# Where the tiles of a matmul begin in their partition: two paddings in a ten-layer kernel

## The chip, the cores and the metric

The kernel runs on one core of one Trainium2 chip. The metric is the device time of a run in microseconds (us), lower being better; the time given for a kernel is the median of several runs. A matmul here takes one operand that is held in the array (stationary, loaded by a weight load, "PEld" in the profile) and one that streams through it (moving). Both come from SBUF, whose 128 partitions each hold a row of bytes; a tile has the same byte address in every partition, and this document is about that address.

## The reference

A sequence of 256 tokens of width 1024 goes through two blocks of two layers each. Everything is float32.

```python
x = first_block(x, ...)    # 2 x (rmsnorm, mixer, + x; rmsnorm, swiglu, + x)
                           #   layer 0: gated spatial mixing beside latent attention
                           #   layer 1: retention with four heads
x = second_block(x, ...)   # 2 x (swiglu with 4096, layer norm; hybrid mixer, layer norm; swiglu, layer norm)
# hybrid mixer: a gated delta rule behind a causal convolution of 4 taps,
# a chunked attention with a relative bias, and a sliding-window attention with sinks,
# each gated and projected, then one output projection
```

Almost all of the arithmetic is in products of the 256 tokens with large weight matrices.

## The kernel before, in words

The work is a chain of ten stages: the two mixers and two feed-forwards of the first block, then feed-forward, hybrid mixer, feed-forward twice for the second. The order of the work is written out by hand; there is no loop on the chip. The same code runs once without a chip to record which slabs of weights are needed in which order, and then again to emit the instructions.

Each float32 product is made of three fast ones: both operands are split in two parts, "hi" (rounded to the fast format float32r) and "lo" (the rest), and `mm3` (line 230) issues hi x hi, hi x lo and lo x hi into the same PSUM tile. All matmuls go through `mm` (line 227), so all of them have line 228 in the profile; transposes through `tr` (line 235, 236 in the profile).

The weights stream in units of up to 1 MB. `prep` (line 135) loads each half of a unit into a tile "raw" through SyncE's DMA queue, has ScalarE round it into "hi" and VectorE subtract into "lo"; up to four units are ahead of their use, on four buffers each of hi and lo.

The activations stand transposed in two tiles "xh" and "xl" of 8 x 256 (`new_xT`, line 427), one pair per stage. Products appear in three forms:
- features by tokens (`pair_tiles`, line 339, and `chunk` in `ffn`, line 587): the weights are stationary, 256 columns of xh or xl move. In the hybrid mixer the branch projections use the same form with the branch's own transposed output, a tile "s", moving.
- tokens by features (`block`, line 284): xh or xl is stationary, up to 512 columns of weights move.
- the second matrix of a feed-forward and the output projections (`emit_down`, line 616, `outlast`, line 370): a pair of tiles "s" is stationary, 512 columns of weights move into four PSUM tiles "acc".

Attention, retention and the delta rule use plain float32 matmuls on smaller tiles between these.

SBUF is handed out from pools, in the order in which `build` (line 1530) opens them. The constants come first (`consts`, line 1512): the identity (512 bytes of each partition), the masks (3584), a column of -0.5 (64) and "colt", the small per-feature columns, 196 numbers wide (784 bytes). Then the weights' pool with hi, lo and raw, then the pool of the working tiles, then xh and xl. In the working pool `tile` (line 204) picks the smallest of six sizes; all of a size stand together, in the order in which the sizes are first used: 4096 bytes (11 of them), 64 (24), 2048 (22), 1088 (4), 256 (10), 2080 (2). The last, "s2x", are used by the convolution of the hybrid mixer alone (`cb_conv`, line 1095), which takes 518 numbers of one. The allocator rounds each tile up to a multiple of 32 bytes; the first constant stands at byte 16512. The profile strips the digits from the names, so the sizes "s4", "s2", "s1" all appear as "s", and "s2x" as itself.

Of the kernel before, what the change touches and what calls it, by code (L numbers as in the profile page):

```python
# [4 lines left out]
F32 = mybir.dt.float32  # L5
# [10 lines left out]
HEAD = 2  # L16
TAIL = 3
ACC = 4


class Nothing:
# [94 lines left out]
class Net:  # L116
# [13 lines left out]
        self.hold = False  # L130
        self.pend = {}

    # weight stream

    def prep(self):
        i = self.made
# [62 lines left out]
        self.nc.sync.dma_start(t, self.dram[name][:, o:o + n])  # L199
        return t  # L200

    # tiles

    def tile(self, *free, dt=F32):
        n = int(np.prod(free))
        for tag, size, bufs in (("c", 16, 24), ("c2", 64, 10), ("s1", 272, 4), ("s2", 512, 22), ("s2x", 520, 2), ("s4", 1024, 11)):
            if n <= size:
                break
        else:
            raise ValueError(n)  # L210
        t = self.sp.tile([128, size], dt, tag=tag, bufs=bufs, name=tag)
        t = t[:, 0:n]
        if len(free) == 2:
            t = t.rearrange("p (a b) -> p a b", a=free[0])
        elif len(free) == 3:
            t = t.rearrange("p (a b c) -> p a b c", a=free[0], b=free[1])
        return t
# [4 lines left out]
    def work(self):  # L222
        return self.pp.tile([128, 512], F32, tag="work", bufs=8 - ACC, name="work")

    # short forms

    def mm(self, out, l, r, start=True, stop=True):
        self.nc.tensor.matmul(out, lhsT=l, rhs=r, start=start, stop=stop)  # L228
# [43 lines left out]
        self.nc.gpsimd.tensor_tensor(out=out, in0=out, in1=self.nh[:, 0:n], op=ALU.pow)  # L272

    def bc(self, a, m):
        """[128, n] -> [128, n, m] with a stride of zero"""
        return a.unsqueeze(2).to_broadcast([128, a.shape[1], m]) if not self.recording else a

    def bh(self, a, h):
        """[128, n] -> [128, h, n] with a stride of zero"""
        return a.unsqueeze(1).to_broadcast([128, h, a.shape[1]]) if not self.recording else a  # L280

    # products with streamed weights

    def block(self, b, n, units, xT, cb):
        ps = self.acc() if self.gacc else self.work()
# [10 lines left out]
        yield  # L296

    def group(self, n, units, xT, cb):
        """out[token, n columns] of x @ w, one block of tokens after the other"""
        self.need_x(1)  # L300
        for b in range(2):
            yield from self.block(b, n, units, xT, cb)
        self.pump()

    def opening(self, groups):
        """the first groups of a stage: the second block of tokens comes late"""
        groups = [(n, self.col_units(key, cols), cb) for n, key, cols, cb in groups]
        self.need_x(0)
        for b in range(2):
            for n, units, cb in groups:  # L310
                for i, _ in enumerate(self.block(b, n, units, self.xT, cb)):
                    if b == 0 and i == 0 and units is groups[-1][1]:
                        self.need_x(1)
                    yield

    def col_units(self, key, cols, K=8, per=4):
        """cols: column ranges, or a function of the inputs that gives the [K * 128, n] slab"""
        units = []
        n = sum(c1 - c0 for c0, c1 in cols)
        for k in range(0, K, per):  # L320
            def fn(inp, k=k):
                return kslab2(key(inp), k, k + per, *cols)
            units.append(self.unit((per, n), fn) + (per,))
        return units
# [3 lines left out]
        yield from self.group(n, self.col_units(key, cols, K, per), self.xT, cb)  # L328

    def apair(self, key, cols, cb):  # L330
        """out[feature, token] of x @ w for two tiles of features"""
        def fn(inp):
            return kslab2(key(inp), 0, 8, *cols)
        u = self.unit((8, 256), fn)
        self.need_x(1)
        yield from self.pair_tiles(u, 0, self.xT, 8, cb)
        self.pump()
# [10 lines left out]
        yield  # L348

    def outproj(self, key, r0, xT, y, first, last, K=4, per=2):  # L350
        """y[block][half] += x @ w for K tiles of the rows of w from r0"""
        units = []
        for k in range(0, K, per):
            def fn(inp, k=k):
                return kslab(key(inp), r0 + k, r0 + k + per, 0, 1024)
            units.append(self.unit((per, 1024), fn))
        for b in range(2):
            for k in range(K):
                hi, lo = units[k // per]
                for n in range(2):  # L360
                    self.mm3(y[b][n], tuple(t[:, k, 128 * b:128 * b + 128] for t in xT),
                             (hi[:, k % per, 512 * n:512 * n + 512], lo[:, k % per, 512 * n:512 * n + 512]),
                             first and k == 0, last and k == K - 1)
                if k % 2 == 1 and k < K - 1:
                    yield ("part", b)
            if b == 1:
                self.pump()
            yield ("block", b)

    def outlast(self, key, r0, xTs, y, first):  # L370
        """y += x @ w for the last rows of w, four tiles per item of xTs; in the last units the first block of tokens comes first"""
        n = 2 * len(xTs)

        def unit(i):
            return self.unit((2, 1024), lambda inp: kslab(key(inp), r0 + 2 * i, r0 + 2 * i + 2, 0, 1024))

        def emit(i, b, w):
            xT = xTs[i // 2]
            xT = xT() if callable(xT) else xT
            for k in range(2):  # L380
                for h in range(2):
                    self.mm3(y[b][h], tuple(t[:, 2 * (i % 2) + k, 128 * b:128 * b + 128] for t in xT),
                             (w[0][:, k, 512 * h:512 * h + 512], w[1][:, k, 512 * h:512 * h + 512]),
                             first and i == 0 and k == 0, i == n - 1 and k == 1)
        for i in range(n - TAIL):
            w = unit(i)
            for b in range(2):
                emit(i, b, w)
                if b:
                    self.pump()  # L390
                yield ("part", b)
        ws = {}
        for b in range(2):
            for i in range(n - TAIL, n):
                if b == 0:
                    ws[i] = unit(i)
                    if i == n - TAIL:
                        self.pump()
                        self.hold = True
                emit(i, b, ws[i])  # L400
                yield ("block", b) if i == n - 1 else ("near" if b and i == n - 2 else "part", b)

    def to_T(self, src, b, dst, n, k0=0):
        """src [128 tokens, n * 128] into dst hi/lo [128, k, 256]"""
        for q in range(0, n, 4):
            m = min(4, n - q)
            ps = self.work()
# [2 lines left out]
            p = ps[:, 0:128 * m].rearrange("p (k t) -> p k t", k=m)  # L410
# [3 lines left out]
    def pair(self, n):  # L414
        return self.tile(n, 256, dt=F32R), self.tile(n, 256, dt=F32R)

    # ends of stages

    def need_x(self, b):
        for i in range(b + 1):  # L420
# [81 lines left out]
        self.pend[b] = post  # L502

    def finish_out(self, b, y):
        """the last layer norm: squares about the mean of the first half, the second half comes last"""
        c = self.how[3]
        z, h, junk = self.tile(1024), self.tile(1024), self.tile(1024)
        sm, q, nm0, nm, dm, e, r = (self.tile(n) for n in (2, 2, 1, 1, 1, 1, 1))
# [34 lines left out]
        for _ in gen:  # L543
            pass

    # the two-matrix gated feed-forward

    def ffn(self, nt, gate, up, down, nxt):
        """gate, up: (fn of inputs -> matrix, first column); down: fn -> matrix"""
        C = nt // 2  # L550
        self.gacc = False
        y = self.new_y()
# [70 lines left out]
        hp, late = head()  # L623
        for c in range(C):
# [3 lines left out]
            if HEAD <= c <= C - TAIL:  # L628
                for e in range(0 if c == HEAD else c - 1, c):
                    w = unit_down(e)  # L630
# [17 lines left out]
                        emit_down(c, b, w, (j,))  # L648
            self.finish(b, y[b])

    # softmax over the last axis of [128, H, K]

    def softmax(self, s, H, K, scale, sink=None):
        """scale: a number, or one per row and head (positive)"""
        nm = self.tile(H)
        self.nc.vector.tensor_reduce(out=nm, in_=s, axis=AX.X, op=ALU.max)
        if sink is not None:
# [17 lines left out]
        return p  # L675

    def p_T(self, p, H, nk):
        """p [128 q, H, nk * 128] -> [128 k, H, nk, 128 q]"""
        pT = self.tile(H, nk, 128)
        flat = pT.rearrange("p a b c -> p (a b c)")  # L680
        for i in range(0, H * nk, 4):
# [7 lines left out]
                self.vcp(flat[:, 128 * i:128 * i + 512], ps)  # L689
        return pT  # L690

    # layer 0 of the first block

    def even(self, nxt):
        self.gacc = True
# [78 lines left out]
        vv = [self.tile(8, 64) for _ in range(2)]  # L774

        def rope(x, b, H, dst):
            """x [128, H, 32]"""
            r = rt1 if b else rt
            pool = self.nc.gpsimd
            t = self.tile(H, 32)  # L780
# [165 lines left out]
        run(fill, 1)  # L946
        self.tail(fill, y)

    # layer 1 of the first block

    def odd(self, nxt):
        w_in = lambda inp: inp["odd_w_in"][0]
# [86 lines left out]
        g = self.outlast(lambda inp: inp["odd_w_out"][0], 8, [oT[2], lambda: oT[3]], y, False)  # L1039
        self.tail(halfway(g, 3, lambda: E(3)), y)  # L1040

    # the mixer of the second block

    def hyb(self, l, nxt):
        nc = self.nc
# [212 lines left out]
        def task_a():  # L1258
            while "kvc" not in events:
                yield "wait"  # L1260
            M = self.masks
            # beta and g
            beta, g = self.tile(2, 4), self.tile(2, 4)
            while "qc" not in events:
                yield "wait"
# [23 lines left out]
                self.mul(t, self.bh(M["U"], 4), self.bc(g[:, b], 128))  # L1289
                gU.append(t)  # L1290
            yield
            # k in token layout, normalised; v in token layout; the lengths of q
            kt, vt, rq = [None] * 2, [None] * 2, [None] * 2

            def lengths(ps):
# [26 lines left out]
                nc.vector.tensor_reduce(out=rq[b], in_=by_head(sq), axis=AX.X, op=ALU.add)  # L1322
                nc.gpsimd.tensor_scalar(out=rq[b], in0=rq[b], scalar1=128e-6, scalar2=128e-12, op0=ALU.mult, op1=ALU.add)
            yield
            # decays: from j to i in [i, j], below the diagonal times beta and with the diagonal
            Dx, DT = [None] * 2, [None] * 2
            for b in range(2):
                ps = self.work()
# [33 lines left out]
                at[b] = DT[b]  # L1362
                self.mul(at[b], DT[b], ps)
            yield
            # inverse of I + A: blocks of four in closed form, then doubled; X = inverse, Y = its transpose
            X, Y, Q = ([self.tile(512) for _ in range(2)] for _ in range(3))
            idb = self.bh(self.ident, 4)
            B, IB, C = Q, X, Y
# [138 lines left out]
        y = self.new_y()  # L1507
        self.tail(self.outlast(lambda inp: inp["w_out_2"][l], 0, mT, y, True), y)

    # the whole  # L1510

    def consts(self):
        nc = self.nc
# [6 lines left out]
        self.nh = self.cp_.tile([128, 16], F32, name="nh")  # L1520
        nc.gpsimd.memset(self.nh, -0.5)
        if not self.recording:
            self.colt = self.cp_.tile([128, max(self.collay.n, 1)], F32, name="colt")

    def late_consts(self):
        nc = self.nc
# [121 lines left out]
```

## Time and profile before

| | |
|---|---|
| runs | 2352.81, 2352.85, 2354.22 us; median 2352.85 us |
| span of the profiled execution (first to last instruction) | 2348.7 us |
| the time of the profiled execution itself | not listed apart from its span; the median of the runs is 4.15 us above the span |
| busy: PE, PEld, DVE, ACT, POOL | 99%, 91%, 59%, 46%, 4% |
| matmuls and weight loads | 15966 each |
| DMA | 419.51 MB, mean 179 GB/s |

PE is the matmul engine, PEld its weight loads, DVE VectorE, ACT ScalarE, POOL GpSimd. A matmul's busy time is longer than the distance from its start to the next one's, because matmuls are pipelined: the distances tell what a matmul costs, not the mean duration. The profile's order of the two inputs in a name is that of the alphabet and doesn't tell which is stationary; the shape does, with the code.

### The profile page before, as it was taken

The page shows a single profiled execution, that of the slowest core. Times are in us where ns is not written, and L with a number is a line of the kernel's source. Part 1 is how long each engine was busy: PE and PEld are TensorE (multiplying, and loading weights), DVE is VectorE, ACT ScalarE, POOL GpSimd, SP SyncE. Part 2 cuts the span into 40 slices and gives each one's busy share as a digit, 9 for nine tenths or more (in the row PEclk, how much of TensorE's full clock was granted, in tenths as well). Part 3 has the DMA queues.
Part 4 walks back from the last instruction along what each step waited for, and adds up shares of the span by engine and source line. Part 5 has one row for each costly group of instructions (what it writes and reads, how often), then busy time and mean ns, then how long its engine had stood idle before and what let it go on. Part 6 is the DMA issues. An engine that isn't in the chain of part 4 may idle for free.

```text
span 2348.7 us, 38487 instructions
## 1 busy us (share of the span) xinstructions
PE 2323.6 (99%) x15966; PEld 2140.5 (91%) x15966; DVE 1393.4 (59%) x1764; ACT 1087.6 (46%) x1530; POOL 92.5 (4%) x149
## 2 busy tenths in 40 slices
PE   8999999999999999999999999999999999999998
PEld 7789988889989999999998999899999999989997
DVE  6654475565455454786666454655457875664544
ACT  6644344354444444564445444444445544453433
POOL 4200000000000000000000000000000000000000
PEclk9999999999999999999999999999999999999999
DMA  7465555555556555553365555555555533665552
GB/s 244 139 206 189 189 193 173 191 170 190 192 171 217 195 184 176 185 174 118 105 201 199 194 183 193 182 201 189 188 181 185 186 105 107 189 206 188 189 189 90
DMA packets 120575, 419.51 MB, mean 179 GB/s; under 512 B 14408, under 2 KB 17224, under 8 KB 120400
## 3 DMA queue, kind: packets, MB, share of 16 engines
q1 hardware_dynamic: 120112, 416.53, 53.7%
q8 instruction: 125, 2.05, 0.3%
q10 hardware_dynamic: 288, 0.52, 0.1%
q14 instruction: 50, 0.41, 0.1%
HBM read 415.95 MB, written 1.05 MB: 178 GB/s over the span
## 4 chain that ended last, share of the span: by engine, by line
PE 97%; DVE 1%; POOL 1%; ACT 0%; DMA 0%; issue 0%; SPq 0%; POOLq 0%; DVEq 0%; ACTq 0%
PE work L228 52%; PE acc L228 42%; PE work L236 2%; DVE lo L148 0%; DMA raw<-in_w 0%; POOL c L271 0%; ACT hi L147 0%; DVE s L251 0%; POOL c L828 0%; POOL c L827 0%; POOL c L272 0%; DVE s L239 0%; PE work L1412 0%; ACT s L258 0%; DVE xl L239 0%
## 5 line engine op out<-in xcount | busy, mean ns | idle before, releaser
L148 DVE TENSOR_TENSOR lo<-raw,hi 128x1024 fp32r<-128x1024 f32 (+3 forms) x772 | 918.3, 1209 | 564.0 <-ACT hi L147 562.3
L147 ACT CAST hi<-raw 128x1024 fp32r<-128x1024 f32 (+3 forms) x772 | 783.4, 1037 | 922.2 <-issue 667.3
L228 PE MATMUL work<-xh,hi 128*128 128x256 f32 x2496 | 699.2, 280 | 0.0
L228 PE MATMUL work<-xl,hi 128*128 128x256 f32 x2496 | 696.5, 279 | 0.0
L228 PE MATMUL work<-xh,lo 128*128 128x256 f32 x2496 | 696.4, 279 | 0.0
L228 PE MATMUL acc<-hi,s 128*128 128x512 f32 (+1 forms) x1736 | 553.4, 391 | 0.0
L228 PEld LDWEIGHTS work<-xh,hi 128*128 128x128 f32 x2496 | 468.5, 188 | 2.7
L228 PEld LDWEIGHTS work<-xl,hi 128*128 128x128 f32 x2496 | 467.1, 187 | 2.7
L228 PEld LDWEIGHTS work<-xh,lo 128*128 128x128 f32 x2496 | 469.1, 188 | 0.0
L228 PEld LDWEIGHTS acc<-hi,s 128*128 128x128 f32 x1736 | 325.7, 188 | 65.8 <-ACT s L261 0.3
L228 PE MATMUL acc<-lo,s 128*128 128x512 f32 (+1 forms) x868 | 337.6, 389 | 0.0
L228 PE MATMUL acc<-xh,hi 128*128 128x256 f32 x800 | 227.5, 284 | 0.0
L228 PE MATMUL acc<-xl,hi 128*128 128x256 f32 x800 | 223.9, 280 | 0.0
L228 PE MATMUL acc<-xh,lo 128*128 128x256 f32 x800 | 223.7, 280 | 0.0
L228 PEld LDWEIGHTS acc<-lo,s 128*128 128x128 f32 x868 | 163.1, 188 | 30.6
L239 DVE TENSOR_TENSOR s<-s,work 128x512 f32<-128x512 f32 (+1 forms) x128 | 81.0, 636 | 172.3 <-PE work L228 160.9
L228 PEld LDWEIGHTS acc<-xh,hi 128*128 128x128 f32 x800 | 150.2, 188 | 0.8 <-issue 0.5
L228 PEld LDWEIGHTS acc<-xl,hi 128*128 128x128 f32 x800 | 150.1, 188 | 0.7 <-issue 0.5
L228 PEld LDWEIGHTS acc<-xh,lo 128*128 128x128 f32 x800 | 150.2, 188 | 0.2
L228 PE MATMUL work<-hi,xh 128*128 128x512 f32 x320 | 128.6, 402 | 0.2 <-ACT xh L261 0.2
L228 PE MATMUL work<-hi,xl 128*128 128x512 f32 x320 | 126.6, 396 | 0.5 <-DVE xl L239 0.5
L228 PE MATMUL work<-lo,xh 128*128 128x512 f32 x320 | 126.5, 395 | 0.0
(117 smaller groups left out, 1949.8 us busy)
## 6 DMA issues: line engine op xcount, KB each, us to landing
raw<-in_w SPq DMA_DIRECT2D x748, 512.0 KB, 4.3
s<-in_rows SPq DMA_DIRECT2D x16, 512.0 KB, 7.4
raw<-in_w SPq DMA_DIRECT2D x12, 288.0 KB, 3.4
s<-in_rows SPq DMA_DIRECT2D x9, 256.0 KB, 5.0
raw<-in_w SPq DMA_DIRECT2D x4, 384.0 KB, 6.8
raw<-in_w SPq DMA_DIRECT2D x4, 256.0 KB, 4.4
s<-in_relb SPq DMA_DIRECT2D x2, 512.0 KB, 4.3
raw<-in_w SPq DMA_DIRECT2D x4, 240.0 KB, 2.5
```

Of the source, the lines that this page charges most:

```text
L147: self.nc.scalar.copy(hi[:, a:b], raw)
L148: self.nc.vector.tensor_tensor(out=lo[:, a:b], in0=raw, in1=hi[:, a:b].bitcast(F32), op=ALU.subtract)
L228: self.nc.tensor.matmul(out, lhsT=l, rhs=r, start=start, stop=stop)
L236: self.nc.tensor.transpose(out, src, self.ident)
L239: self.nc.vector.tensor_tensor(out=out, in0=a, in1=b, op=op)
```

## The change

Two paddings, and comments taken out. The tile for the columns of constants is made wider, up to the next multiple of 512 bytes behind the constants, and only its first part is used, as before. The two buffers of the convolution are made 24 numbers wider. No instruction is added, dropped or moved.

```diff
+LINE = 512
+FIRST = 16512
...
-    # weight stream
+
...
     def tile(self, *free, dt=F32):
         n = int(np.prod(free))
-        for tag, size, bufs in (("c", 16, 24), ("c2", 64, 10), ("s1", 272, 4), ("s2", 512, 22), ("s2x", 520, 2), ("s4", 1024, 11)):
+        for tag, size, bufs in (("c", 16, 24), ("c2", 64, 10), ("s1", 272, 4), ("s2", 512, 22), ("s2x", 544, 2), ("s4", 1024, 11)):
             if n <= size:
                 break
...
         if not self.recording:
-            self.colt = self.cp_.tile([128, max(self.collay.n, 1)], F32, name="colt")
+            fixed = 512 + 3584 + 64 + FIRST
+            self.colt = self.cp_.tile([128, max(self.collay.n, 1) + -(fixed + 4 * self.collay.n) % LINE // 4], F32, name="colt")[:, 0:max(self.collay.n, 1)]
```

## Rows read from the trace of the kernel before

**Rows 1.** The page's opening, busy time by engine, and granted clock in 40 slices.
```profile
span 2348.7 us, 38487 instructions
...
PE 2323.6 (99%) x15966; PEld 2140.5 (91%) x15966; DVE 1393.4 (59%) x1764; ACT 1087.6 (46%) x1530; POOL 92.5 (4%) x149
...
PEclk9999999999999999999999999999999999999999
```

**Rows 2.** PE's waits, longest in total first: us in total, times, longest.
```profile
PE work L236 <- DVE s L251: 10.0, 4, 8.7
PE work L228 <- DVE s L251: 4.0, 1, 4.0
PE work L236 <- POOL s L829: 1.1, 1, 1.1
```

**Rows 3.** The chain in order of time: start us, us, what, xcount.
```profile
143.54 5.45 PE work L228 x48
...
159.89 11.31 PE work L228 x96
...
260.61 22.61 PE work L228 x192
283.22 15.00 PE acc L228 x66
...
2324.13 16.37 PE acc L228 x72
```

**Rows 4.** Groups of PE's instructions, shapes apart: tile<-inputs, shape, xcount | busy us, mean ns.
```profile
L228 PE MATMUL work<-xh,hi 128*128 128x256 f32 x2496 | 699.2, 280 | 0.0
...
L228 PE MATMUL acc<-hi,s 128*128 128x512 f32 x1712 | 546.4, 392 | 0.0
L228 PE MATMUL acc<-lo,s 128*128 128x512 f32 x856 | 333.5, 390 | 0.0
L228 PE MATMUL acc<-xh,hi 128*128 128x256 f32 x800 | 227.5, 284 | 0.0
...
L228 PE MATMUL work<-hi,xh 128*128 128x512 f32 x320 | 128.6, 402 | 0.2 <-ACT xh L261 0.2
...
L228 PE MATMUL acc<-s,hi 128*128 128x256 f32 x384 | 70.5, 285 | 0.0
L228 PE MATMUL acc<-s,lo 128*128 128x256 f32 x192 | 54.5, 284 | 0.0
L228 PE MATMUL acc<-hi,xh 128*128 128x512 f32 x80 | 32.5, 406 | 0.0
```

**Rows 5.** PE's timeline, a branch projection: start us, us, operation, xcount.
```profile
1173.19 0.40 PE L228 MATMUL acc<-s,hi 128*128 128x256 f32 x2
...
1183.62 0.40 PE L228 MATMUL acc<-s,hi 128*128 128x256 f32 x2
```

**Rows 6.** PE's timeline, column groups of the odd layer.
```profile
309.96 0.39 PE L228 MATMUL work<-lo,xh 128*128 128x512 f32 x1
...
323.49 0.39 PE L228 MATMUL work<-hi,xl 128*128 128x512 f32 x1
```

**Rows 7.** PE's timeline, a 264-column group of the hybrid mixer and the next matmul.
```profile
955.52 0.28 PE L228 MATMUL acc<-hi,xh 128*128 128x264 f32 x1
...
958.42 0.39 PE L228 MATMUL acc<-hi,xh 128*128 128x512 f32 x1
```

## The prediction, made before the result was known

> **What bounds the kernel now.** I read the page's first block, then the waits of PE, then the chain of waits in order of time, the groups of PE's instructions with their shapes kept apart, and last PE's timeline in three short stretches.
>
> [...] PE's largest wait is 10.0 us in all, its next 4.0 us [rows 2]. Nearly the whole span is therefore matmuls back to back, and the time is the sum of the distances from one matmul's start to the next. DVE (59%) and ACT (46%) have room, and no wait of PE names a DMA.
>
> The chain gives these distances, since it counts the matmuls of an unbroken stretch: 96 in 11.31 us and 192 in 22.61 us are 117.8 ns each, 48 in 5.45 us are 113.5 ns each, 66 in 15.00 us and 72 in 16.37 us are 227.3 ns each [rows 3]. The first two kinds are 256 columns wide, the last kind 512.
>
> The timeline adds two more. With a tile "s" against "hi" and "lo" at 256 columns (the branch projections), the 87 matmuls from 1173.19 to 1183.62 take 10.43 us, 119.9 ns each [rows 5]. With 512 columns of "hi" or "lo" moving and xh or xl stationary (the column groups of the odd layer), the 58 from 309.96 to 323.49 take 13.53 us, 233.3 ns each [rows 6].
>
> So the same shape costs 117.8 or 119.9 ns, and 227.3 or 233.3 ns, in steady runs. What differs is where the operands lie. From the program's allocation (constants from byte 16512, tiles rounded up to 32 bytes) I work out each tile's start modulo 512: 16512 + 512 + 3584 + 64 + 784 = 21456, rounded to 21472, is 480. All that follows in the pools in multiples of 512 keeps 480: hi, lo, raw, the 4096-byte and the 2048-byte tiles. Behind the four 1088-byte and the two 2080-byte tiles xh and xl start at 210208, which is 288. Slices that a matmul takes are whole multiples of 512 bytes apart, save in the 264- and 288-column units, so a tile's start holds for all of its slices. Moving start minus stationary start is then:
> - 256 columns, xT moving over a weight: 288 - 480 = -192, at 117.8 ns (rarely 113.5)
> - 256 columns, s moving over a weight: 0, at 119.9 ns
> - 512 columns, weight moving over s: 0, at 227.3 ns
> - 512 columns, weight moving over xT: +192, at 233.3 ns
>
> It isn't the accumulator that makes the difference: the 72 matmuls of the last feed-forward stay in one PSUM tile for 18 in a row, the 66 change it after three, and both run at 227.3 ns [rows 3].
>
> **The change part by part.** *The constants.* colt grows from 784 to 832 bytes, so the weights' pool begins at 21504 and hi, lo, raw, s4 and s2 start at 0 instead of 480. *The convolution buffers.* Two tiles grow from 2080 to 2176 bytes; with the four of 1088 they now fill 17 times 512, and xh and xl start at 210432, which is 0 as well. The instructions stay the same in number, shape and order: the load of colt still writes 196 columns, the convolution still uses 518 columns of its tile, no queue and no wait changes, and the stripped comments are nothing. These parts cost 0; what hides even a small change in them is that PE waits for none of these tiles [rows 2]. All the effect there can be is in the matmuls' distances.
>
> *What the matmuls' distances become.* After the change moving and stationary start at the same place everywhere: distance 0, which the trace has in both shapes, only 32 bytes lower in the 512. I take the rows at distance 0 as the nearest:
> - xT moving, 256 columns: 3 x 2496 + 3 x 800 = 9888 matmuls [rows 4]. Five runs of 48 like that in rows 3 and two of 24 are at 113.5 ns, 288 in all; the other 9600 are at 117.8. At 119.9 they cost 9600 x 2.1 ns = +20.2 us and 288 x 6.4 ns = +1.8 us.
> - s moving, 256 columns: 384 + 192 [rows 4], stay at 119.9: 0.
> - s stationary, 512 columns: 1712 + 856 [rows 4], stay at 227.3: 0.
> - xT stationary, 512 columns: 3 x 320 + 3 x 80 = 1200 [rows 4], from 233.3 to 227.3: 1200 x 6.0 ns = -7.2 us.
>
> The sum is +14.8 us, all on the path, since PE has no slack. It is made against the profiled execution: 2348.7 + 14.8 = 2363.5 us of span. Around its span that execution has what the other runs have too: their median of 2352.85 lies 4.15 us above the span, which I carry over unchanged. That gives 2352.85 + 14.8 = 2367.7 us.
>
> *Bounds.* No row shows distance 0 with both starts at 0 of 512, so the price of a 256-column matmul is open between two ends. From below: 227.3 - 119.9 = 107.4 ns is what 256 further columns cost at the same distance, so 12.5 ns of each matmul at distance 0 are not streaming; were all of this gone, and what xT's have on top, it would be 9600 x 10.4 + 288 x 6.1 + 576 x 12.5 + 2568 x 12.5 + 1200 x 18.5 ns = 163 us less. From above: every 512-column matmul at the 233.3 ns of rows 6, and the 256s at 119.9, is 2568 x 6.0 = +15.4 us and no -7.2 us: 14.8 + 15.4 + 7.2 = +37 us. I take the rows at distance 0, since they are the same instructions at the distance that the change sets.
>
> [...]
>
> **A further hint on what matters.** In the 264-column groups the slices of hi and lo lie 1056 bytes apart, so the moving start runs through 480, 0, 32 and 64 over xT's 288. The 24 matmuls from 955.52 to 958.42 take 2.90 us, 120.8 ns [rows 7]; less 8 columns at 107.4 / 256 ns that is 117.4, about the 117.8 of the others. Half of them already start at a multiple of 64, one in four at 0 of 512. An aligned moving start by itself does not show a gain. The stationary start is never aligned in the trace.
>
> **The rivals.**
> 1. *Aligned starts are cheaper in themselves* (faster). A load of 512 bytes that begins at 480 or 288 touches two pieces of 512, at 0 one. If the extra piece is what costs, the 256s may settle at 113.5 ns, the quickest that rows 3 show, and xT's 512s at 227.3: 9600 x 4.3 + 576 x 6.4 + 1200 x 6.0 ns = 41.3 + 3.7 + 7.2 = 52.2 us less, 2301 us. For it: the 113.5 exist at the same starts, so the extra is avoidable. Against: s and xT touch equally many pieces and yet cost differently, and the 264s show nothing.
> 2. *Only the 512s follow the distance*; the 117.8 of the 256s is set by the weight load and stays: -7.2 us, 2345.7 us. For it: the weight load is busy for 91% of the span [rows 1], and a 256-column matmul has little more time than its load. Against: 119.9 with the same load.
> 3. *No effect*, the differences come from something other than starts: 2352.85 us. Against: rows 5 and 6.
> 4. *Slower still*: at 0 both streams hold each other up and the 512s settle at 233.3 everywhere, the upper bound above: 2352.85 + 37 = 2390 us. It decides from the first feed-forward on. Against: 227.3 is steady at distance 0.
>
> **How the numbers follow.** Forecast 0.45, rival 1 0.28, rival 2 0.09, rival 3 0.10, rival 4 0.08. The forecast's own range is 2361 to 2374 us (0.5 ns of reading on 9888 matmuls and a few us of settling at each switch). Rival 1 may come with anything from a quarter of its gain to the full bound, so the range is 2300 to 2386: it leaves out the lower half of rival 1 and most of rival 4. Within 0.2% (4.7 us) is what a measurement can't tell from no change. Faster: rivals 1 and 2, 0.37; same: rival 3, 0.10; slower: forecast and rival 4, 0.53.
>
> **What would show it.** In the chain after, stretches of 96 should take 11.5 us instead of 11.31, those of 66 still 15.0 us; the odd layer's 512s against xT should be at 227 ns, and no run at 113.5 should be left. Rival 1 shows as 96 in 10.9 us or less. If the 66s leave 15.0 us, the place in the 512 counts and not the distance alone, and the step "nearest rows" is wrong. If nothing moves in any of these stretches, rival 3 holds. Any change in the waits of PE beyond a few us would mean that something other than the starts was changed.

## The result and the profile after

The changed kernel takes 2368.36 us (median of four runs, 2367.84 to 2369.13) against 2352.99 us for the kernel before (four runs, 2352.81 to 2354.22): a ratio of 1.0064, with a 95% interval of 1.0050 to 1.0079. It is slower by 15.4 us; 2367.7 was forecast.

The opening of the page, after: span, busy time by engine, granted clock in 40 slices.

```profile
span 2365.8 us, 38487 instructions
...
PE 2340.4 (99%) x15966; PEld 2163.8 (91%) x15966; DVE 1393.5 (59%) x1764; ACT 1087.7 (46%) x1530; POOL 92.7 (4%) x149
...
PEclk9999999999999999999999999999999999999999
```

Against [rows 1] the instruction counts are equal, DVE, ACT and POOL are within 0.2 us, and the granted clock is again at nine tenths or more in all slices. Only PE and PEld grew, by 16.8 and 23.3 us.

The waits of PE, after: us in total, times, longest.

```profile
PE work L238 <- DVE s L253: 10.5, 3, 9.4
PE work L230 <- DVE s L253: 4.0, 1, 4.0
PE work L238 <- POOL s L831: 1.2, 1, 1.2
```

With [rows 2] these make 0.6 us more. So nearly all of the loss lies inside the unbroken stretches of matmuls.

The chain in order of time, after: start us, us, what, xcount.

```profile
144.89 5.75 PE work L230 x48
...
161.55 11.51 PE work L230 x96
...
263.43 23.03 PE work L230 x192
286.46 14.99 PE acc L230 x66
...
2341.33 16.36 PE acc L230 x72
```

Line by line against [rows 3]: 48 matmuls went from 5.45 to 5.75 us (113.5 to 119.8 ns each), 96 from 11.31 to 11.51 (117.8 to 119.9), 192 from 22.61 to 23.03; the 66 and the 72 of 512 columns did not move.

PE's timeline after, in the column groups of the odd layer (the same 58 matmuls as [rows 6]):

```profile
313.01 0.40 PE L230 MATMUL work<-lo,xh 128*128 128x512 f32 x1
...
326.17 0.39 PE L230 MATMUL work<-hi,xl 128*128 128x512 f32 x1
```

13.16 us instead of 13.53: 226.9 ns each instead of 233.3. The branch projections, after, the same 87 matmuls as [rows 5]:

```profile
1180.57 0.40 PE L230 MATMUL acc<-s,hi 128*128 128x256 f32 x2
...
1191.01 0.40 PE L230 MATMUL acc<-s,hi 128*128 128x256 f32 x2
```

10.44 us, 120.0 ns each: unchanged.

For the balance I took all start-to-start distances of a kind from both traces, leaving out those above 148 ns (256 columns) and 276 ns (512 columns), which hold a wait or another instruction:

| kind | number | before, ns | after, ns | sum |
|---|---|---|---|---|
| 256 columns, xT moving over a weight | 9820 | 117.68 | 119.92 | +22.0 us |
| 512 columns, weight moving over xT | 1154 | 233.35 | 227.83 | -6.4 us |
| 512 columns, weight moving over s | 2536 | 227.85 | 227.63 | -0.6 us |
| 256 columns, s moving over a weight | 560 | 119.89 | 119.90 | 0 |

Together +15.0 us; the medians differ by 15.4 us. The two spans differ by 17.1 us. What is more lies mostly in three places outside the table: the first matmul starts at 9.45 us instead of 8.66 (+0.8 us); behind PE's wait of 4.0 us in the first stage the granted clock is 0.50 for 6.8 us instead of 3.4, and 1.00 on both sides of it (+0.9 us); and the 384-column matmuls of the first stage take 0.7 us more. Smaller groups give 0.3 us back. The profiled execution of before was probably also a quick one, which is an estimate: where a run's time stands beside its own span it is 2.6 us above it (2368.41 and 2365.8 here; 2353.0 and 2350.4 for the kernel before in a later run), while the 2348.7 us of [rows 1] lie 4.15 us below the median.

### The profile page after: what moved, and what is told of

It reads as the page before. It is cut to its first block, busy times and chain, and to the rows that moved or that the text cites. A ratio compares the mean times of both kernels' runs of the same rounds, so it can differ in the third digit from the quotient of the medians.

```text
span 2365.8 us, 38487 instructions
## 1 busy us (share of the span) xinstructions
PE 2340.4 (99%) x15966; PEld 2163.8 (91%) x15966; DVE 1393.5 (59%) x1764; ACT 1087.7 (46%) x1530; POOL 92.7 (4%) x149
## 4 chain that ended last, share of the span: by engine, by line
PE 97%; DVE 1%; POOL 1%; ACT 0%; DMA 0%; issue 0%; SPq 0%; POOLq 0%; DVEq 0%; ACTq 0%
PE work L230 52%; PE acc L230 42%; PE work L238 2%; DVE lo L150 0%; DMA raw<-in_w 0%; POOL c L273 0%; ACT hi L149 0%; DVE s L253 0%; POOL c L830 0%; POOL c L829 0%; POOL c L274 0%; DVE s L241 0%; PE work L1414 0%; DVE xl L241 0%; ACT s L260 0%
## 5 line engine op out<-in xcount | busy, mean ns | idle before, releaser
L230 PE MATMUL work<-xh,hi 128*128 128x256 f32 x2496 | 706.7, 283 | 0.0
L230 PE MATMUL work<-xh,lo 128*128 128x256 f32 x2496 | 706.4, 283 | 0.0
L230 PE MATMUL work<-xl,hi 128*128 128x256 f32 x2496 | 706.3, 283 | 0.0
L230 PEld LDWEIGHTS work<-xl,hi 128*128 128x128 f32 x2496 | 478.7, 192 | 2.7
L230 PEld LDWEIGHTS work<-xh,hi 128*128 128x128 f32 x2496 | 478.7, 192 | 2.7
L230 PEld LDWEIGHTS work<-xh,lo 128*128 128x128 f32 x2496 | 478.7, 192 | 0.0
L230 PE MATMUL acc<-xl,hi 128*128 128x256 f32 x800 | 226.7, 283 | 0.0
L230 PE MATMUL work<-s,s 128*128 128x128 f32 (+8 forms) x884 | 122.5, 297 | 4.0 <-DVE s L253 4.0
```

## Experiments

The forecast's theory is called *distance*: what counts is the moving operand's start minus the stationary one's. Its first rival is *place*: what counts is where in 512 bytes each start lies. All kernels are built from the changed kernel, by one to four lines each; the short forms of long lines in the diffs below show only what differs. "x" stands for xh and xl; x at 64 means that both begin at 64 modulo 512, and all other operands at 0 unless it is said. The means are taken as in the table above.

**1. The constants' padding alone** (weights and s at 0, x at 320).

```diff
-("s2x", 544, 2)
+("s2x", 520, 2)
```

> Only the constants' padding: hi, lo and all tiles s start at 0 of 512, xh and xl at 320, so that xT minus weight is 320, which is -192 modulo 512, as before the change. Distance theory (the price of a matmul follows from moving start minus stationary start alone): everything as before the change, 2353 us (2351 to 2355), 96 matmuls in 11.31 us, xT's 512-column matmuls at 233.3 ns. Place theory (a start at 0 of 512 has a price of its own, whatever the other operand does): the 256-column matmuls keep the 119.9 ns of the changed kernel since their weights begin at 0, xT's 512s go back to 233.3: 2368 + 7 = 2375 us.

2352.68 us, ratio 0.9997 (0.9988 to 1.0007). The chain of this kernel:

```profile
160.09 11.31 PE work L230 x96
...
260.81 22.61 PE work L230 x192
283.43 15.01 PE acc L230 x66
```

Every weight and every s is now aligned, and the stretches are those of [rows 3] to 0.01 us. Its timeline in the odd layer, 57 matmuls from first to last start:

```profile
310.16 0.39 PE L230 MATMUL work<-lo,xh 128*128 128x512 f32 x1
...
323.46 0.40 PE L230 MATMUL work<-lo,xh 128*128 128x512 f32 x1
```

13.30 us, 233.3 ns each: also as before [rows 6]. Aligning everything but x did nothing; place, which gave 2375 us, is wrong.

**2. The convolution's padding alone** (all operands at 480, none aligned).

```diff
-            self.colt = self.cp_.tile([128, max(self.collay.n, 1) + -(fixed + 4 * self.collay.n) % LINE // 4], F32, name="colt")[:, 0:max(self.collay.n, 1)]
+            self.colt = self.cp_.tile([128, max(self.collay.n, 1)], F32, name="colt")[:, 0:max(self.collay.n, 1)]
```

> Only the convolution buffers' padding: every tile, xh and xl too, starts at 480 of 512; nothing is aligned, and all distances are 0. Distance theory: as the changed kernel, 2368 us (2366 to 2370), 96 in 11.51 us, xT's 512s at 227.3 ns. Place theory: 480 is as misaligned as before, so as before, 2353 us and 11.31 us.

2369.29 us, ratio 1.0064 (1.0047 to 1.0081). The chain of this kernel:

```profile
145.30 5.75 PE work L230 x48
...
161.96 11.51 PE work L230 x96
...
263.84 23.03 PE work L230 x192
286.88 14.99 PE acc L230 x66
```

These are the durations of the whole change, to 0.01 us, with no tile at a multiple of 512. Over the whole trace the 256s of xT take 119.92 ns on average, xT's 512s 227.95. The whole loss comes from the 192 bytes by which the convolution's buffers push x.

They push x against the weights, but also against "raw", which ScalarE and VectorE read while PE works. The two traces tell these apart: the 256s beside which neither engine worked on "raw" take 117.72 ns before and 119.84 after, those beside which one or both did 117.63 to 117.67 and 119.96 to 119.98. So the 2 ns do not come from the other engines' work on the weights.

**3 and 4. How far does the distance count?** x at 64 and at 128.

```diff
-("s2x", 544, 2)
+("s2x", 552, 2)        # x at 64
+("s2x", 560, 2)        # x at 128
```

> The changed kernel with the convolution buffers 32 numbers wider than before the change instead of 24: xh and xl at 64 of 512, all else at 0. Distance theory with a period of 256 bytes: 64 is the same as -192, so 117.8 ns for the 256s and 233.3 ns for xT's 512s, 2353 us. Distance theory with a period of 512: a distance that no row has; on a straight line through 117.8 at -192 and 119.9 at 0 it is 120.6 ns, and 225 ns for the 512s, 2372 us. Place theory: 2368 us or more.

> xh and xl at 128 of 512, all else at 0. No row has this distance. Distance theory with a straight line: 121.3 ns for the 256s, 223 ns for xT's 512s, 2377 us. [...] Place theory: 2368 us.

x at 64, one run: 2351.76 us beside 2353.42 for the kernel before.

```profile
160.58 11.31 PE work L230 x96
...
283.92 15.01 PE acc L230 x66
```

Means of 117.67 and 233.34 ns, as with x at 320 (117.70 and 233.38): in this pair the price repeats after 256 bytes. So the kernel before stood at distance 64 of 256 (in experiment 1's terms 320 - 256; in the prediction's, -192), and 192 for the 512s.

x at 128, one run: 2371.61 us, expected 2377 by the straight line, 2368 by place.

```profile
162.46 11.52 PE work L230 x96
```

The 256s are at 119.61 ns, back at nearly the price of distance 0, and the 512s at 232.4. Neither of the two gave both.

**5 to 9. The rest of the circle**, with a pad ahead of xh and xl in their pool.

```diff
+self.xp.tile([128, 8], F32, tag="pad", bufs=1, name="pad")   # 32 bytes; 24: 96, 40: 160, 48: 192, 56: 224
```

> xh and xl at 32 of 512, all else at 0. Smooth theory (the price of a matmul is a smooth function of the distance, with a period of 256 bytes): between the neighbours at 0 and 64, 118.9 ns for the 256s and 230 ns for xT's 512s, 2360 us. Step theory (what counts is which pieces of the memory both streams meet in, so neighbours say nothing): anything from 113.5 to 123 ns for the 256s, 2310 to 2400 us, and a value more than 0.5 ns from the middle of its neighbours.

> xh and xl at 96 of 512, all else at 0. Smooth theory: between the neighbours at 64 and 128, 118.7 ns for the 256s and 232.9 ns for xT's 512s, 2361 us. Step theory: anything from 113.5 to 123 ns, more than 0.5 ns from that middle.

> xh and xl at 192 of 512, all else at 0: the mirror of 64, so that xT's 512-column matmuls have the distance -192, the one that the 256s have in the kernel before. Smooth theory: between the known 128 and 256, 119.8 ns for the 256s, 229.9 ns for xT's 512s, 2370 us. [...] Step theory: anything else.

> xh and xl at 224 of 512, all else at 0. Smooth theory: near the price at 256, 119.9 ns for the 256s and 228.6 ns for xT's 512s, 2369 us. Step theory: more than 0.5 ns away from that.

> xh and xl at 160 of 512, all else at 0: the last of the eight distances. Smooth theory: between its neighbours at 128 and 192, 118.1 ns for the 256s and, for xT's 512s at distance 96, between the known 64 and 128, 231.0 ns: 2354 us. Step theory: more than 0.5 ns away from that middle.

One run each: x at 32 2342.32 us, at 96 2375.4, at 192 2334.17, at 224 2360.52 (the kernel before beside them: 2354.26), and at 160 2360.04 (beside 2352.1). A stretch of 96 in each of the five chains, in this order:

```profile
160.88 11.20 PE work L230 x96
```

```profile
160.75 11.52 PE work L230 x96
```

```profile
158.97 11.31 PE work L230 x96
```

```profile
162.34 11.36 PE work L230 x96
```

```profile
161.27 11.40 PE work L230 x96
```

The mean prices, by distance modulo 256 bytes, in ns (the 512s of a kernel stand at 256 minus the distance of its 256s; the period of 256 rests on the one pair 64 and 320):

| distance | 0 | 32 | 64 | 96 | 128 | 160 | 192 | 224 |
|---|---|---|---|---|---|---|---|---|
| 256 columns, x over a weight | 119.9 | 116.8 | 117.7 | 120.0 | 119.6 | 118.5 | 116.6 | 118.3 |
| 512 columns, weight over x | 227.8 | 233.3 | 229.6 | 233.4 | 232.4 | 234.1 | 233.3 | 233.2 |

The smooth curve that I had laid through the first points was missed four times (2360 expected for x at 32, 2361 for 96, 2370 for 192, 2369 for 224); at 160 its 118.1 for the 256s came within 0.5 ns, but its 231.0 for the 512s was off by 2.4. The step theory's claim, more than 0.5 ns off the middle for the 256s, held in four of the five, but it named no value and is not shown by that: the pieces of memory it speaks of were a guess that no run shows, and the highest mean of the 256s is 120.0 ns where its range went to 123. Where x stands decides, by no rule that these runs show: neighbours 32 bytes apart differ by up to 5.5 ns, and the two shapes have their lowest prices at different distances. That only the distance counts, and not x's own place, is shown for the distances 0 and 64 (experiments 1 to 3); at the other six only one place was tried.

**10 and 11. One weight tile moved**: lo at 64, with hi, s and x at 0. "raw" stands behind lo and moves to 64 with it; no matmul reads it.

```diff
+        if i == 0:
+            self.wp.tile([128, 16], F32, tag="pad1", bufs=1, name="pad1")     # ahead of lo
...
+        if i == 0:
+            self.wp.tile([128, 112], F32, tag="pad2", bufs=1, name="pad2")    # behind it
```

> The changed kernel with lo alone at 64 of 512 (hi, s, xh and xl at 0). The 256-column matmuls come in threes: xh over hi, xl over hi, xh over lo; x minus lo is 192 modulo 256, a distance at which the 256s took 116.6 ns, x minus hi is 0, at 119.9. While the second streams, the weight load of the third (lo) runs. Next-load theory (the stream of a matmul and the load for the next one hold each other up): the distance from the second's start to the third's falls to about 116.6 ns, first and third stay at 119.9. Own-weight theory (what counts is a matmul's own stationary): the third falls, first and second stay. Both: a mean of 118.8 ns, -10 us; the 512s with lo moving go to about 229.6 ns, +3 us: 2361 us. If neither place matters for lo: 2368 us.

2850.91 us in one run, and its page tells why it says nothing of distances:

```profile
span 2848.3 us, 38487 instructions
...
PEclk8777777777777777777777777777777777777777
```

The granted clock was 0.752 over the whole span, while the kernel before ran beside it on the same chip at 0.999 (2352.1 us). So the same kernel was run again.

> The kernel of the run before once more, whose granted clock stood at 0.75 from beginning to end, so that it told nothing of distances. Next-load theory: the second 256-column matmul of each three (xl over hi, while the load of lo runs) falls to about 116.6 ns, first and third stay at 119.9; own-weight theory: the third (xh over lo) falls, the others stay. Both 2361 us; 2368 us if lo's place does not matter.

2361.57 us (2360.54 to 2362.57), ratio 1.0034 (1.0021 to 1.0047). The chain:

```profile
162.05 11.31 PE work L234 x96
...
263.29 22.62 PE work L234 x192
285.91 15.31 PE acc L234 x66
...
2334.02 16.72 PE acc L234 x72
```

The total is about the 2361 that both readings gave, but by other terms. I had expected the price to change for those matmuls of a triple alone that have lo, or that run while lo is being loaded. All three fell: xh over hi is at 117.65 ns, xl over hi at 117.53, xh over lo at 118.31, though the first two stream at distance 0 over their own weights and the first does so while another load at distance 0 runs (the overlap shows in the changed kernel: an xl over hi starts at 161.50 us, the load for the xh over lo behind it at 161.51). And the 512s over s, two thirds of which use only hi and s at distance 0, all rose to 232 ns (66 in 15.31 us). The terms are 9820 x 0.15 + 2536 x 4.1 - 1154 x 1.35 - 576 x 1.9 = 1.5 + 10.4 - 1.6 - 1.1 = +9.2 us against before; the medians differ by 7.9. That "raw" moved too is not the cause: the 256s beside which neither ScalarE nor VectorE worked on it take 117.85 ns, the others 117.80 to 117.83. In this run, then, the price belonged to the sequence of loads and streams and not to the pair alone.

**12. x at 192, timed.**

> The quickest of the distances once more, now timed in rounds. If the one look of 2334 us was the kernel's own time: 2334 us (2332 to 2336), 0.8% below the kernel before, 1.4% below the changed one, with the 256s at 116.6 ns of which a quarter stand at 113.3. If the quick stretches at 113.3 come and go from run to run: between 2334 and 2344 us, which is the time with all of them at 117.6.

2336.0 us (2334.76 to 2337.49) against 2353.69 for the kernel before: ratio 0.9925 (0.9913 to 0.9938). It beats the kernel before by 0.75% and the changed one, by the medians, by 1.4%, with 192 bytes of padding more than the changed one has. The time lies at the upper edge of the first expectation and inside the second. Its chain, with a stretch of the odd layer (96 matmuls against x and 8 others) between the usual ones:

```profile
160.16 11.31 PE work L230 x96
...
260.64 22.61 PE work L230 x192
283.26 14.97 PE acc L230 x66
...
371.50 12.20 PE work L230 x104
```

The stretches of 96 are those of before. The gain of the 256s lies elsewhere: the stretch of 104 takes 12.20 us. In the changed kernel the chain has the same stretch as

```profile
375.61 12.83 PE work L230 x104
```

and 0.63 us over its 96 is 6.6 ns each, so these run at 113.3 ns. In the timeline of the kernel with x at 192, 90 matmuls lie between these two starts:

```profile
371.46 0.28 PE L230 MATMUL work<-xl,hi 128*128 128x256 f32 x1
...
381.66 0.28 PE L230 MATMUL work<-xl,hi 128*128 128x256 f32 x1
```

10.20 us, 113.3 ns each. About a quarter of all its 256s run like this (2487 of them), the rest at 117.7, with every start at the same place modulo 512. So the 116.6 of the table is the mean of two cadences, and no steady stretch runs at it. Against before the sums are 9820 x 1.03 + 1154 x 3.93 + 2536 x 0.98 ns = 10.1 + 4.5 + 2.5 = 17.1 us less; the medians differ by 17.7.

Experiments 7 and 12 are one kernel, run twice, so their traces show which of it repeats. Of 127 unbroken stretches of 12 or more 256s, 121 have the same cadence in both. Six switched, in both directions. One of them, first in experiment 7, then in 12:

```profile
142.62 5.46 PE work L230 x48
```

```profile
143.63 5.66 PE work L230 x48
```

The same instructions on the same tiles took 113.8 ns each in one run and 117.9 in the other. The second expectation, that quick stretches come and go, holds for these few; most stay.

The traces also show where the 0.98 ns of the 512s over s go. Before, 24 of them between two stretches of 256s take 5.48 us: the first seven take 224 to 241 ns each, from the eighth on all are at 227. With x at 192 all 24 are at 227 from the first, 5.44 us in all. In the kernel before, then, PE's cadence takes some seven matmuls to settle after the switch from one form of product to the other, and with x at 192 none.

## Why the prediction was right

- *PE alone bounds, and its time is a sum of distances.* Right: counts, waits (within 0.6 us) and the other engines are as before, and the sum over three kinds of matmul gives 15.0 of the 15.4 us.
- *Moving minus stationary start makes the difference.* Right in what it was used for, and shown by experiments 1 and 2: alignment without a change of distance does nothing (0.9997), and the change of distance without alignment does all of it (1.0064). With nothing but x moved, experiment 2 takes 15.9 us more than the kernel before (2369.29 against 2353.42).
- *The price at distance 0 is that of the rows at distance 0.* Right, to 0.1 ns for the 256s (119.9 forecast, 119.92 found) and 0.5 ns for the 512s (227.3 forecast, 227.83 as the mean of all). What carried it is more than the distance of one pair: in the rows used as nearest, hi, lo and s all start at the same place, as all operands do after the change. Experiment 11, where lo alone among them starts elsewhere, shows that a pair at distance 0 does not keep its price then. The prediction did not see this condition, so in that part it was fortunate.
- *+20.2 and +1.8 us for xT's 256s.* +22.0 measured. The number was 9820 instead of 9888 and the old price 117.68 on average; no run at 113.5 was left, as forecast (5.75 us for the 48).
- *-7.2 us for xT's 512s.* -6.4: 1154 undisturbed distances instead of 1200, and 5.5 ns instead of 6.0.
- *The 4.15 us around the span.* This was mis-sized: 2.6 us lie around a span, and the other 1.55 would be the profiled execution's lead over the median. The sum is a difference, so the forecast of the time did not suffer, but the span forecast, 2363.5, is 2.3 us short.
- *The lower bound's 12.5 ns of each matmul that are not streaming.* Not borne out. The bound took what 256 further columns cost from a 256-column price that is not the quickest. In the quickest stretches 256 columns take 113.3 ns (experiment 12) and 512 take 226.7 (24 in 5.44 us), twice as much, so they show no such fixed part. The forecast did not use the bound.
- *Rival 1, aligned starts are cheaper*: would have shown as 96 in 10.9 us; it is 11.51, and experiment 1 refutes it directly. *Rival 2, only the 512s follow*: refuted by the same line; that a 256-column matmul has little more time than its load is not shown either, for before a load is recorded at 187 to 188 ns, with one such matmul every 117.7 ns. *Rival 3, no effect*: refuted. *Rival 4, the 512s over s rise as well*: they stayed at 14.99 us for 66 here, but experiment 11 shows that they can rise, to 15.31.

What the prediction had too simple: "distance" carried it because it forecast a distance that the trace already held in both shapes. For other distances the idea gave no number (experiments 4 to 9), and experiment 11 changed matmuls whose own distance had not changed. What stays open is the mechanism: the runs show that the relative starts decide, that the prices repeat after 256 bytes in the one pair tried (64 and 320), and that a stretch can hold one of two steady cadences at the same starts; whether reads hold each other up, and which, they do not show. That the s-stationary 512s fall by 1 ns with x at 192 (227.85 to 226.87) is traced to the matmuls after a switch between the forms of product (experiment 12), but why these settle at once there is open too.

## What to carry to other kernels

Where PE is back to back, compare the start-to-start distances of equal shapes across the kernel; if they differ in steady runs, tabulate the operands' start bytes before touching anything, and take prices only from stretches in which all operands stand to each other as they will. Aligning to a round number was not in itself good here: it brought every pair to distance 0, a dear one for the 256-column matmuls of which this kernel has ten thousand (119.9 ns each instead of 117.7). A pad of 32 to 224 bytes ahead of one operand was a cheap knob here, and better swept on the chip than reasoned out: between the best and the worst of eight places lay 41 us, 1.8% (single runs; the best was timed again in experiment 12).

## What the runs showed of the hardware that was not expected

- In this kernel the cadence of float32r matmuls changes with where x starts relative to the other operands: means of 116.6 to 120.0 ns for 256 columns and 227.8 to 234.1 ns for 512, and not smoothly (the table of experiments 5 to 9). Alignment to 512 bytes by itself changed nothing (experiment 1, ratio 0.9997).
- The same instructions with the same starts hold 113.3 ns in one stretch and 117.7 in another for dozens of matmuls on end, and a few stretches switch between the two from one run of a kernel to the next (experiment 12; rows 3 have the same pair in the kernel before).
- A switch from the 256s of x to the 512s over s leaves its mark for some seven matmuls in the kernel before, 224 to 241 ns each until they settle at 227, and none with x at 192 (experiment 12).
- At the quickest cadence 512 columns cost twice what 256 cost, 226.7 and 113.3 ns (experiment 12).
- One whole run on one core was granted 0.752 of the clock, 2850.91 us, with the kernel before at 0.999 beside it; the same kernel, later and on another chip, had 0.998.
